# Loading the first x of a batched matmul: two row tiles in one buffer, and other pieces for the DMA engines

## Chip, cores, metric

The kernel runs on one core of a Trainium2 chip. The metric is the device time of one execution in microseconds (us). A run of this program on one core has no second core or die beside it to compare with; all runs below are listed as fast.

## What is computed

```python
batch, m, k, n = 32, 512, 1024, 768
x:      float32 [32, 512, 1024]
weight: float32 [32, 1024, 768]
out = np.matmul(x, weight)         # float32 [32, 512, 768]
```

Reading and writing this once is 167.8 MB in and 50.3 MB out.

## The kernel before

Weights and all x but the first are cast to bf16 by the DMA itself, on a queue that POOL issues (queue 0 in the profile). The first x comes as float32 on the queue of SP (queue 1), in two buffers: three row tiles in one transfer, the fourth tile in seventeen pieces. The tile is 128 partitions, one row of 4 KB in each.

```python
x_first = x_pool.tile([P, MT - 1, K], F32, name="x_sb")
x_fourth = one_pool.tile([P, 1, K], F32, name="one_sb")
nc.sync.dma_start(x_first, x_view[0, :, :MT - 1])
few = [slice(at, first + 20, 4) for first in (0, 20, 40) for at in range(first, first + 4)]
for rows in (slice(64, 96), slice(96, 112), slice(112, P), slice(60, 62), slice(62, 64), *few):
    nc.sync.dma_start(x_fourth[rows, 0], x_view[0, rows, MT - 1])
load_w(0)
# ... identity
load_pair(1); load_w(1); load_w(2); load_pair(3)
```

Each entry of `few` is a transfer of five rows. A transfer of five rows runs on fewer DMA engines than one of 128 (the prediction cites the page for this and shows packets that come in fives), so the pieces set how much each DMA engine carries.

The order of work in a batch: x is transposed on PE, DVE copies the transposed tile from PSUM, PE multiplies, ACT and DVE take the result out, POOL issues the store. Before batch b POOL issues the weights of batch b + 3, and must wait there until PE has done with the buffer that they go to.

```python
for b in range(B):
    if b % 2 and b + AHEAD + 1 < B:
        load_pair(b + AHEAD + 1)       # cut: the last one
    if b % 2 and 2 < b < B - HELD - AHEAD:
        store((b - 3) // 2)
    if b + AHEAD < B:
        load_w(b + AHEAD)
    # ... transposes
    for pair in range(2):              # two row tiles each
        for half in range(2):
            mt = 2 * pair + half
            if mt not in xT:
                xT[mt] = transpose_first(mt)     # batch 0: the late tiles
            matmuls(pm, half, xT[mt], b, range(KT), False)
        evacuate(b, pair, pm)
```

## Time and profile before

| | before |
|---|---|
| time, three runs | 514.83 us (514.74 to 515.25); the profiled run, a fourth, 514.44 |
| span in the profile | 512.7 us |
| PE busy | 435.4 us |
| sum of PE's three waits for DMA | 55.6 us (26.2 for weights, 19.1 and 10.3 for the first x) |

The lines behind this table stand in the prediction. How to read them: in the windows, the column before the last is the mean busy share of the sixteen DMA engines (it reads 1.02 to 1.03 over long stretches here, as packets of one engine overlap a little), and the last is what they moved. A packet is counted whole in the window in which it starts. In a window of 1 us, about as long as one packet of queue 0, the share is therefore rough; at the end of the run, where packets take 0.23 us, it is good. A share of one engine alone is 1/16, or 0.06.

A second reading comes from the packet records that the trace keeps: start, length, size and queue of every DMA packet, without the number of the engine. Each transfer ends on each engine that it ran on with a completion packet of 4 bytes. The last transfers of the kernel are even over all engines, eight packets of 6,144 bytes on each, so the completions of one engine follow each other at 1.85 us, and a completion with none 1.85 us after it is the end of one engine. I call these times the finishes. They are worked out from the records by that rule. The shares of the last windows check them: a finish at 508.4 us takes 0.6 of a sixteenth off the window from 508 to 509.

### The profile page before, as it was taken

How to read it: one execution, taken by the hardware profiler on the slowest of the kernel's cores; microseconds unless marked ns; L12 is line 12 of the kernel's file. 1: busy time of each engine (PE TensorE's matmuls, PEld its weight loads, DVE VectorE, ACT ScalarE, POOL GpSimd, SP SyncE). 2: the span in 40 equal slices, each digit the busy share in tenths (PEclk: the TensorE clock that was granted, in tenths of full speed). 3: DMA queues.
4: the chain of work that ended last, by engine and by line, in shares of the span. 5: the costliest groups of instructions: out<-in, count | busy, mean ns of one | idle time of the engine just before them, and what ended most of it. 6: DMA issues, size and time to landing. Idle time of an engine off the chain costs nothing.

```text
span 512.7 us, 5785 instructions
## 1 busy us (share of the span) xinstructions
PE 435.4 (85%) x2576; PEld 278.7 (54%) x2576; DVE 130.0 (25%) x196; ACT 76.1 (15%) x129; POOL 39.1 (8%) x73
## 2 busy tenths in 40 slices
PE   1806999999999996997989989798898989999991
PEld 1504666666666663654646546464464645666660
DVE  0202324141515141320413205041040410514121
ACT  1100121212121201111111111111101111120201
POOL 3000010101010101001010000101001000010000
PEclk9956999999999998997999989899798998999997
DMA  8999999999999999999999999999999999999998
GB/s 240 224 221 213 218 220 216 333 221 310 243 218 336 215 324 231 228 325 220 330 223 234 318 223 334 217 247 304 221 333 218 258 295 220 331 215 212 320 427 345
DMA packets 12712, 135.63 MB, mean 265 GB/s; under 512 B 1296, under 2 KB 1296, under 8 KB 3088
## 3 DMA queue, kind: packets, MB, share of 16 engines
q0 software_dynamic: 11440, 126.88, 96.6%
q1 hardware_dynamic: 1248, 8.39, 4.1%
q8 instruction: 20, 0.33, 0.2%
q14 instruction: 4, 0.03, 0.0%
HBM read 167.77 MB, written 50.33 MB: 425 GB/s over the span
## 4 chain that ended last, share of the span: by engine, by line
PE 46%; DMA 37%; issue 8%; DVE 5%; another core or an unknown queue 1%; POOL 1%; ACT 0%; SPq 0%; POOLq 0%
PE pm L123 40%; DMA w_sb<-in_weight_dram 28%; DMA one_sb<-in_x_dram 8%; PE pt L78 5%; DVE xT L85 4%; DVE out_sb L144 1%; POOL out_dram L164 0%; PE pt L105 0%; POOL w_sb L70 0%; POOL x_sb L60 0%; DVE one_sb L144 0%; DVE xT L93 0%; ACT out_sb L145 0%; SPq L151 0%
## 5 line engine op out<-in xcount | busy, mean ns | idle before, releaser
L123 PE MATMUL pm<-w_sb,xT 128*128 128x256 bf16 (+1 forms) x2048 | 353.7, 336 | 26.4 <-DMA w_sb<-in_weight_dram 26.2
L123 PEld LDWEIGHTS <-xT 128*128 128x128 bf16 x2048 | 205.3, 101 | 170.3 <-DMA w_sb<-in_weight_dram 29.3
L144 DVE COPY out_sb<-pm 128x512 f32<-128x512 f32 x62 | 42.9, 691 | 317.6 <-PE pm L123 317.6
L78 PE MATMUL pt<-ident,x_sb 128*128 128x128 f32 x496 | 79.8, 302 | 10.5 <-DVE xT L85 10.2
L78 PEld LDWEIGHTS pt<-ident,x_sb 128*128 128x128 f32 x496 | 69.3, 209 | 21.5 <-DVE xT L85 18.7
L85 DVE COPY xT<-pt 128x1024 bf16<-128x1024 bf16 x120 | 77.4, 687 | 11.0 <-PE pt L78 11.0
L143 ACT COPY out_sb<-pm 128x512 f32<-128x512 f32 x62 | 36.3, 585 | 271.7 <-PE pm L123 271.7
L145 ACT COPY out_sb<-pm 128x512 f32<-128x512 f32 x62 | 36.3, 585 | 145.7 <-PE pm L123 145.6
L70 POOL DMA_DIRECT2D w_sb<-in_weight_dram x37 | 20.1, 544 | 404.8 <-PE pm L123 397.6
L105 PE MATMUL pt<-ident,one_sb 128*128 128x128 f32 x8 | 1.9, 421 | 19.1 <-DMA one_sb<-in_x_dram 19.1
L106 DVE CAST xT<-pt 128x512 bf16<-128x512 f32 x8 | 5.8, 733 | 34.6 <-PE pt L105 34.1
L105 PE MATMUL pt<-ident,x_sb 128*128 128x128 f32 x24 | 5.3, 383 | 10.5 <-DMA x_sb<-in_x_dram 10.3
L105 PEld LDWEIGHTS pt<-ident,one_sb 128*128 128x128 f32 x8 | 1.6, 219 | 19.4 <-issue 19.4
L164 POOL DMA_DIRECT2D out_dram<-out_sb x14 | 10.1, 719 | 6.7 <-ACT out_sb L143 3.5
L105 PEld LDWEIGHTS pt<-ident,x_sb 128*128 128x128 f32 x24 | 4.1, 209 | 11.5 <-issue 10.3
L60 POOL DMA_DIRECT2D x_sb<-in_x_dram x15 | 8.1, 539 | 10.9 <-DMA w_sb<-in_weight_dram 10.9
L144 DVE COPY one_sb<-pm 128x512 f32<-128x512 f32 x2 | 1.4, 690 | 9.0 <-PE pm L123 9.0
L93 DVE COPY xT<-pt 128x1024 bf16<-128x1024 bf16 x4 | 2.6, 686 | 0.2 <-PE pt L78 0.2
L143 ACT COPY one_sb<-pm 128x512 f32<-128x512 f32 x2 | 1.2, 585 | 6.4 <-PE pm L123 6.4
L145 ACT COPY one_sb<-pm 128x512 f32<-128x512 f32 x2 | 1.2, 585 | 1.6 <-PE pm L123 1.6
L143 ACT ACT_TABLE_LOAD x1 | 1.3, 1283 | 0.7 <-PEq L232 0.7
L64 POOL DMA_DIRECT2D x_sb<-in_x_dram x1 | 0.5, 528 | 2.1 <-DMA w_sb<-in_weight_dram 2.1
(6 smaller groups left out, 0.9 us busy)
## 6 DMA issues: line engine op xcount, KB each, us to landing
w_sb<-in_weight_dram POOLq DMA_DIRECT2D x28, 1536.0 KB, 41.7
out_dram<-out_sb POOLq DMA_DIRECT2D x14, 3072.0 KB, 55.3
x_sb<-in_x_dram POOLq DMA_DIRECT2D x15, 2048.0 KB, 49.8
w_sb<-in_weight_dram POOLq DMA_DIRECT2D x7, 768.0 KB, 38.2
out_dram<-out_sb SPq DMA_DIRECT2D x2, 1536.0 KB
x_sb<-in_x_dram SPq DMA_DIRECT2D x1, 1536.0 KB
out_dram<-one_sb SPq DMA_DIRECT2D x2, 768.0 KB
out_dram<-out_sb SPq DMA_DIRECT2D x2, 768.0 KB
```

The source lines that it names most:

```text
L60: nc.gpsimd.dma_start(out=xs[b], in_=pair_view[b // 2])
L70: nc.gpsimd.dma_start(out=ws[b][:, at:at + n, :], in_=w_view[b, :, at:at + n, :])
L78: nc.tensor.transpose(pt[:, j, :], pairs[:, mo, j::JT], ident)
L85: nc.vector.tensor_copy(both[:, :, :, :, half, :].rearrange("p b j i r -> p j b i r"), words(b, mt + MT * half).rearrange("p j (b i r) -> ...
L93: nc.vector.tensor_copy(xT.rearrange("p j m r -> p (j m r)"), words(B - 1, mt).rearrange("p j m -> p (j m)"))
L105: nc.tensor.transpose(pt[:, i, :], rows[:, JT * h + i::KT], ident)
L106: nc.vector.tensor_copy(xT[:, 2 * h:2 * h + 2].rearrange("p j m r -> p j r m"), pt.rearrange("p (j r) m -> p j r m", r=2),)
L123: nc.tensor.matmul(pm[bank][:, at:at + size], xT[:, ko // 2, :, ko % 2], ws[b][:, ko, off:off + size], start=(ko == 0 and not (together an ...
L143: nc.scalar.copy(o[:, 0:512], pm[0])
L144: nc.vector.tensor_copy(o[:, 512:1024], pm[1])
L145: nc.scalar.copy(o[:, 1024:N2], pm[2])
L164: nc.gpsimd.dma_start(out=two_view[at], in_=twos[at])
```

## The change

The first two tiles get a transfer each (a quarter of x[0] is enough for PE to begin), and the last two tiles share one buffer, so that a row of 8 KB can come in one packet. The pieces now are: 80 partitions in transfers of 16 spread partitions (two of five such transfers cut into halves of 4 KB), 8 partitions in one transfer, 40 in transfers of five.

```diff
-        x_first = x_pool.tile([P, MT - 1, K], F32, name="x_sb")
-        x_fourth = one_pool.tile([P, 1, K], F32, name="one_sb")
-        nc.sync.dma_start(x_first, x_view[0, :, :MT - 1])
-        few = [slice(at, first + 20, 4) for first in (0, 20, 40) for at in range(first, first + 4)]
-        for rows in (slice(64, 96), slice(96, 112), slice(112, P), slice(60, 62), slice(62, 64), *few):
-            nc.sync.dma_start(x_fourth[rows, 0], x_view[0, rows, MT - 1])
+        x_first = x_pool.tile([P, 2, K], F32, name="x_sb")
+        x_second = one_pool.tile([P, 2, K], F32, name="one_sb")
+        for mt in range(2):
+            nc.sync.dma_start(x_first[:, mt], x_view[0, :, mt])
+
+        def load_second(rows, *parts):
+            for tiles in parts:
+                nc.sync.dma_start(x_second[rows, tiles], x_view[0, rows, 2:][:, tiles])
+
+        whole, halves = (slice(0, 2),), (slice(0, 1), slice(1, 2))
+        for at in range(5):
+            load_second(slice(48 + at, P, 5), *(halves if at > 2 else whole))
+        load_second(slice(40, 48), *whole)
+        for first in (0, 20):
+            for at in range(first, first + 4):
+                load_second(slice(at, first + 20, 4), *whole)
```

Cut: `rows` in `transpose_first`, which follows the new buffers, and the number of tiles transposed ahead in batch 0, two in place of three.

More of the change, by code (lines that the diff above doesn't have):

```diff
@@ L100, in transpose_first @@
         xT = xT_pool.tile([P, JT, P, 2], BF16, name="xT")
-        rows = x_first[:, mt] if mt < MT - 1 else x_fourth[:, 0]
+        rows = x_first[:, mt] if mt < 2 else x_second[:, mt - 2]
         for h in range(2):
@@ L187 @@
             if b == 0:
-                xT = {mt: transpose_first(mt) for mt in range(MT - 1)}
+                xT = {mt: transpose_first(mt) for mt in range(2)}
             elif b == B - 1:
```

## The prediction

> **What bounds the kernel now.** I read the page first for the engines, slices and queues, then the chain of waits, then windows around both ends, then the waits of the SP queue, and last the single DMA packets that the trace records (start, length, size, queue).
>
> ```profile
> span 512.7 us, 5785 instructions
> PE 435.4 (85%) x2576; PEld 278.7 (54%) x2576; DVE 130.0 (25%) x196; ACT 76.1 (15%) x129; POOL 39.1 (8%) x73
> DMA  8999999999999999999999999999999999999998
> q0 software_dynamic: 11440, 126.88, 96.6%
> q1 hardware_dynamic: 1248, 8.39, 4.1%
> q8 instruction: 20, 0.33, 0.2%
> HBM read 167.77 MB, written 50.33 MB: 425 GB/s over the span
> ```
>
> The DMA row is at 9 in every slice but the first and last, and the shares of queues 0 and 1 sum to over 100%. The sixteen DMA engines are the bound. PE has 15% to spare. The arithmetic agrees: 218.1 MB over 16 engines is 13.63 MB each; a 12,288-byte packet of queue 1 alone takes 460 ns in the packet records, 26.7 bytes per ns; 13.63 MB at that rate is 510 us. So nothing that PE waits for counts unless it leaves a DMA engine without work.
>
> ```profile
> core 0: us, PE busy (x) PEld busy (x) DVE busy (x) ACT busy (x) POOL busy (x), PEclk, DMA share, GB/s
> 0.00:2.00 2.00, 0.00 (x0) 0.00 (x0) 0.00 (x0) 1.26 (x1) 0.93 (x6) 1.00 0.40 68
> 2.00:6.00 4.00, 0.00 (x0) 0.00 (x0) 0.00 (x0) 0.02 (x1) 3.09 (x7) 1.00 0.86 310
> 6.00:43.00 37.00, 13.34 (x73) 8.80 (x74) 5.06 (x7) 1.76 (x3) 0.53 (x1) 0.79 1.03 228
> 43.00:500.00 457.00, 420.29 (x2494) 269.02 (x2495) 123.51 (x187) 70.98 (x122) 34.52 (x60) 0.96 1.02 266
> 508.00:509.00 1.00, 0.00 (x0) 0.00 (x0) 0.00 (x0) 0.00 (x0) 0.00 (x0) 0.50 0.97 406
> 509.00:510.00 1.00, 0.00 (x0) 0.00 (x0) 0.00 (x0) 0.00 (x0) 0.00 (x0) 0.50 0.81 338
> 510.00:511.00 1.00, 0.00 (x0) 0.00 (x0) 0.00 (x0) 0.00 (x0) 0.00 (x0) 0.50 0.47 197
> 511.00:512.70 1.70, 0.00 (x0) 0.00 (x0) 0.00 (x0) 0.00 (x0) 0.00 (x0) 0.50 0.02 7
> ```
>
> These windows show where time can still be had: before 6 us, where the share is low, and after 508 us, where the engines run dry one after the other. In between the share is 1.02. At the end the last completion packets (4 bytes, 9 ns, one per engine) give each engine's own finish: three engines near 508.7 to 509.1 us, seven at 510.14 to 510.54, six at 510.98 to 511.41. Their mean is about 510.5, so a perfect balance would win 0.9 us, 0.2% of the time. That is the whole prize at that end.
>
> ```profile
> PE pt L105 <- DMA one_sb<-in_x_dram: 19.1, 1, 19.1
> PE pt L105 <- DMA x_sb<-in_x_dram: 10.3, 1, 10.3
> ```
>
> Both of these are PE waiting for the first x in the first 43 us (DMA share 1.03 from 6 us on). They look large and cost nothing. The chain of waits runs through the landing of one_sb at 42.9 us, but that chain is a dependency path, and no engine of the bound stands still beside it.
>
> **What the Trainium skill says.** "DMA: Bandwidth & Descriptors", Queues, rings and completion order: each DMA engine takes turns between the queues it has work for, one packet at a time. The trace agrees: on the engines that load the five-row pieces, a 172 ns data packet and a 22 ns completion packet alternate with queue-0 packets of 925 ns. The same page, the section on why a DMA increments its semaphore by 16: the row count fixes how many engines a transfer uses, and on SP it is the lowest-numbered ones; so 16 spread rows go to all sixteen engines, 8 to engines 0 to 7, 5 to engines 0 to 4. The trace agrees on the number: the late 4,096-byte packets come in fives, at 0, 9, 56, 142 and 154 ns; it carries no engine numbers. "Runtime: NRT & Kernel Launch", Instruction fetch mechanics: instructions arrive in blocks of 16 KiB by DMA. The trace has twenty such packets, queue 8, of 880 to 975 ns. Following packets by their phase, these went round eight engines that carry none of the five-row pieces: four engines get three, four get two. That reading is partly ambiguous where two phases meet.
>
> **The balance before.** Rows of x_first are even. The fourth tile puts 18 rows of 4 KB on engines 0 and 1, 16 on 2 to 4, 4 on 5 to 15. A 4 KB packet between queue-0 packets adds 168 ns (172 less 4 of overlap), so engines 0 and 1 carry 14 x 0.168 = 2.35 us more than 5 to 7, and engines 2 to 4 carry 2.0 us more. Fetches add 2 x 0.935 = 1.9 us or 3 x 0.935 = 2.8 us to eight engines, which I take to be 8 to 15. So three engines should be early (5 to 7), seven in the middle (2 to 4 and the four with two fetches), six late (0, 1 and the four with three fetches). These are the counts 3, 7, 6 read above.
>
> **The change, part by part.** No arithmetic changes: the same 8 x 4 transposes, the same copies, and the same POOL order; the SP queue still issues 18 loads at the start. What moves:
>
> - *First two tiles*: 16 packets of 4 KB per engine in place of eight of 12 KB (which held the third tile too). 4 KB alone costs 159 - 4 = 155 ns, so 16 x 0.155 = 2.48 us.
> - *Tiles 2 and 3 in one buffer.* A spread transfer leaves one partition per engine, 8 KB, or two of 4 KB for the two that are halved. An 8 KB packet was not in the trace; between 168 ns for 4 KB and 469 for 12 KB it should add 318 ns (estimate). Engines 0 to 4: 3 x 0.318 + 4 x 0.168 + 9 x 0.318 = 4.49 us; 5 to 7: 3 + 1 of the large, 1.94 us; 8 to 15: 1.63 us. A completion packet adds 3 ns, at most 18 of them.
> - *Sums of the loads of x[0]* after: 7.02 us on engines 0 to 4, 4.45 on 5 to 7, 4.13 on 8 to 15. Before, with 3.67 us for x_first: 6.75 on 0 and 1, 6.41 on 2 to 4, 4.36 on 5 to 15. Differences: +0.27, +0.61, +0.10, -0.23 us.
> - *Where each class then ends:* 0 and 1 from about 511.0 to 511.3; 2 to 4 from 510.1-510.5 to 510.8-511.1; the fetchers with three from 511.2-511.4 to 511.0-511.2; the rest earlier. The last end goes from 511.41 to some 511.2-511.3, a gain of 0.1 to 0.2 us.
>
> *The start.* DMA begins 1.0 us after the first SP issue in both. Until the first queue-0 packet at 6.0 us only queue 1 works, and moved 82 KB per engine there, where 4.2 us at 26.7 bytes per ns would be 110. After: the first two tiles hold 64 KB, and SP issues take 0.25 to 0.77 us, so six pieces (36 KB) are issued by about 5 us: 100 KB, enough. No change expected, within 0.3 us either way.
>
> *Beside the path.* PE needs only the first tile (512 KB) to begin, so its first transpose should come at some 6 us in place of 10.3. The first matmul waits for w[0] and stays near 16 us. Tiles 2 and 3 land when engines 0 to 4 are through: of their 50 turns some 28 are left at 6 us, against 37 of 44 before. 28 queue-0 packets (17 at 0.906, 8 at 1.208, the rest completions) are 25 us, with 94 KB of own data 3.7 us: 34.8 us, and PE goes on at about 35 in place of 42.9. It then has two tiles to transpose and multiply rather than one and a half, so batch 0 ends near 47 in place of 49. As DMA has a backlog there, it gains nothing.
>
> The sum: 514.83 - 0.2 = **514.6 us**.
>
> **The rivals.**
>
> *The earlier landing shortens the run* by the 2 us of batch 0 or the 7 us of PE's wait. For: the chain of waits passes there. Against: the share is 1.02 to 1.03 from 6 to 508 us, so the loads that PE's progress releases only join a queue. It would make 508 to 513. I give it 3%.
>
> *The start starves or small packets lose.* With pieces of one packet per engine issued about every 0.6 us, or with slow first packets (the first twelve took 750 to 1,650 ns in place of 460), all engines could lose 0.3 to 0.8 us before 6 us, and nothing later gives it back. It would make 515.0 to 515.5. Against: the backlog computed above. 20%.
>
> *The balance is better than I think*, if engines 0 to 4 were all in the middle group: then they rise to 510.4-511.1, the fetchers fall by 0.23, and the end is that 0.23 us earlier or slightly more: 514.3 to 514.6. This differs from my path only in the class of engines 0 and 1, which the trace doesn't name.
>
> **Range and chances.** The parts I dispute are each tenths of a microsecond, and three runs of before spread over 0.5 us. So 513.9 to 515.3 should hold it 8 times in 10. A change of 2% is 10 us, ten times what either end has to give: within 2% 0.98, faster 0.01, slower 0.01.
>
> **What would show it.** Right: share at 1.02 between 6 and 508 us; first transpose near 6 us, x_second's wait ending near 35 us; matmuls of batch 0 beginning near 16 us; the last finishes closer together, latest near 511.2, with three early engines still near 509. Wrong: a share under 0.8 between 2 and 6 us (start starved); a latest finish of five engines together after 511.4 (0 to 4 overloaded); a span shorter by over a microsecond, which would mean that PE's wait was paid for somewhere.

## The result

| | before | after |
|---|---|---|
| time, four runs each in the same rounds | 515.03 us (514.74 to 515.25) | 514.97 us (514.78 to 515.75) |
| ratio of the means | | 1.0002 (95%: 0.9985 to 1.0019) |
| sum of PE's waits for DMA | 55.6 us | 56.8 us |
| latest finish of a DMA engine | 511.4 us | 512.6 us (this run), 511.8 us (a second one) |

Ratios are the mean time of one kernel's runs over that of the other's of the same rounds, so not quite the ratio of the medians in the table. The change makes no difference that these runs can show. The profile of the changed kernel is of its slowest run, 515.75 us; the same kernel was profiled a second time, at 514.99 us, among the experiments.

The page of the changed kernel:

```profile
span 514.0 us, 5786 instructions
DMA  8999999999999999999999999999999999999997
q0 software_dynamic: 11440, 126.88, 96.4%
q1 hardware_dynamic: 1472, 8.39, 4.1%
q8 instruction: 20, 0.33, 0.2%
HBM read 167.77 MB, written 50.33 MB: 424 GB/s over the span
```

Queue 1 moves the same 8.39 MB in 224 packets more. The bytes, the bound and the instruction packets are unchanged.

The same windows as in the prediction, of the changed kernel (DMA share and GB/s are the last two columns):

```profile
0.00:2.00 2.00, 0.00 (x0) 0.00 (x0) 0.00 (x0) 1.26 (x1) 0.93 (x6) 1.00 0.07 16
2.00:6.00 4.00, 0.84 (x4) 0.88 (x5) 0.00 (x0) 0.02 (x1) 3.10 (x7) 1.00 1.00 303
6.00:43.00 37.00, 14.48 (x61) 8.53 (x60) 5.07 (x7) 1.17 (x2) 0.53 (x1) 0.68 1.03 231
43.00:500.00 457.00, 417.07 (x2495) 267.56 (x2494) 123.37 (x187) 71.40 (x122) 34.52 (x60) 0.96 1.02 266
509.00:510.00 1.00, 0.00 (x0) 0.00 (x0) 0.00 (x0) 0.00 (x0) 0.00 (x0) 0.50 0.79 332
510.00:511.00 1.00, 0.00 (x0) 0.00 (x0) 0.00 (x0) 0.00 (x0) 0.00 (x0) 0.50 0.57 240
511.00:512.00 1.00, 0.00 (x0) 0.00 (x0) 0.00 (x0) 0.00 (x0) 0.00 (x0) 0.50 0.31 129
```

In the first 6 us the DMA engines were busy for 2 x 0.07 + 4 x 1.00 = 4.14 us on the mean, against 2 x 0.40 + 4 x 0.86 = 4.24 before: the start is neither starved nor better. From 6 to 500 us the share is the same to the digit. At the end it is 0.31 between 511 and 512 us, where before it was nearly gone (0.02 from 511.00 to 512.70): in this run five engines on the mean are still at work in that microsecond.

PE's waits for DMA over the whole run, in us, number, longest; before and then after (two of the three of before stand in the prediction):

```profile
PE pm L123 <- DMA w_sb<-in_weight_dram: 26.2, 8, 4.5
```

```profile
PE pm L123 <- DMA w_sb<-in_weight_dram: 34.9, 10, 5.8
PE pt L105 <- DMA one_sb<-in_x_dram: 16.7, 1, 16.7
PE pt L105 <- DMA x_sb<-in_x_dram: 5.2, 1, 5.2
```

PE begins at 5.2 us in place of 10.3 and the second half lands earlier, so two waits shrink by 7.5 us together. The wait for weights grows by 8.7. In the second profile of the changed kernel the three sum to 55.5 us. This fits a wait that is not the bound: taken away at one place, it comes back at a later load.

The finishes, worked out from the packet records (us from the start of the span; "after, second" is run e1 below):

```
before         508.7 508.7 509.1 | 510.1 510.1 510.2 510.3 510.3 510.5 510.5 | 511.0 511.1 511.1 511.2 511.4 511.4
after          507.6 507.7 508.1 | 509.9 509.9 510.0 510.1 | 511.1 511.4 511.5 511.6 511.6 511.6 511.8 | 512.5 512.6
after, second  507.8 508.2 508.2 | 509.9 510.0 510.2 510.2 510.3 510.6 510.7 510.9 511.1 511.1 511.2 | 511.6 511.8
```

The mean of the sixteen is 510.4, 510.6 and 510.2 us. So in the second run nothing was lost or won in total, and the last engine ends 0.4 us later than before. In the first profiled run there is a disturbance besides: five packets at 121.6 us took 0.7 to 1.0 us longer than their like (x loads of 16,384 bytes, which otherwise take 1,227 ns). The second profile of this kernel has no such group there.

### The profile page after: what moved, and what is told of

Its sections match the earlier page's. It is cut to its first block, busy times and chain, and to the rows that moved or that the text cites. A ratio compares the mean times of both kernels' runs of the same rounds, so it can differ in the third digit from the quotient of the medians.

```text
span 514.0 us, 5786 instructions
## 1 busy us (share of the span) xinstructions
PE 435.9 (85%) x2576; PEld 278.9 (54%) x2576; DVE 129.8 (25%) x196; ACT 76.1 (15%) x129; POOL 39.1 (8%) x73
## 3 DMA queue, kind: packets, MB, share of 16 engines
q1 hardware_dynamic: 1472, 8.39, 4.1%
## 4 chain that ended last, share of the span: by engine, by line
PE 47%; DMA 35%; issue 8%; DVE 5%; another core or an unknown queue 1%; SPq 1%; POOL 1%; ACT 0%; POOLq 0%
PE pm L123 41%; DMA w_sb<-in_weight_dram 29%; DMA one_sb<-in_x_dram 6%; PE pt L78 5%; DVE xT L85 4%; DVE out_sb L144 1%; SPq L156 1%; PE pt L105 0%; POOL out_dram L174 0%; POOL x_sb L60 0%; POOL w_sb L70 0%; SPq L152 0%; DVE xT L106 0%; DVE one_sb L144 0%
## 5 line engine op out<-in xcount | busy, mean ns | idle before, releaser
L78 PE MATMUL pt<-ident,x_sb 128*128 128x128 f32 x496 | 79.8, 302 | 10.4 <-DVE xT L85 10.2
L78 PEld LDWEIGHTS pt<-ident,x_sb 128*128 128x128 f32 x496 | 69.3, 209 | 21.5 <-DVE xT L85 18.7
L105 PE MATMUL pt<-ident,one_sb 128*128 128x128 f32 x16 | 3.0, 350 | 16.7 <-DMA one_sb<-in_x_dram 16.7
L105 PE MATMUL pt<-ident,x_sb 128*128 128x128 f32 x16 | 3.9, 423 | 5.2 <-DMA x_sb<-in_x_dram 5.2
L105 PEld LDWEIGHTS pt<-ident,x_sb 128*128 128x128 f32 x16 | 3.0, 215 | 5.6 <-issue 5.1
## 6 DMA issues: line engine op xcount, KB each, us to landing
x_sb<-in_x_dram SPq DMA_DIRECT2D x2, 512.0 KB
```

The costliest lines, as they stand in the source:

```text
L78: nc.tensor.transpose(pt[:, j, :], pairs[:, mo, j::JT], ident)
L105: nc.tensor.transpose(pt[:, i, :], rows[:, JT * h + i::KT], ident)
```

## The experiments

Theory (balance): sixteen DMA engines are busy from 2 to 508 us; the time is the mean load plus the lead of the engine that ends last, and what the pieces do is to hand out load. Rival 1: PE's wait for the late half of x[0] counts. Rival 2: the many small transfers at the start cost. All kernels below gave correct results. All ratios are to the kernel before, in the same rounds; 515 us times 0.001 is 0.5 us. Where two experiments are compared, it is by these ratios, and their error is that of both.

### The changed kernel again (e1)

Edit: none.

> The changed kernel unaltered, timed beside the three others of this call on one chip. All theories: within 0.5 us of the kernel before (ratio 0.999 to 1.001). Balance theory: per-engine finishes again three early (near 508 to 509 us), four near 510, the rest from 511.1 on.

Measured: 514.99 us (514.91 to 515.41) against 514.61 (514.39 to 515.20) of the kernel before; ratio 1.0009 (0.9996 to 1.0021). The time is as expected. Of the finishes the three early ones are there; the others lie between 509.9 and 511.8 us with hardly a gap, not in the two groups expected. If there is a difference in time, the change is the slower one.

### The wait taken away: one even transfer (e2)

```diff
-        (all pieces of x_second)
+        nc.sync.dma_start(x_second, x_view[0, :, 2:])
```

> Tiles 2 and 3 of the first x come in one transfer of 128 partitions, so all sixteen engines get the same rows, and the piece-wise loading is gone. Balance theory (DMA engines are the bound, the run ends with the last of them): PE's wait for the second half of x[0] shrinks from 16.8 us to under 2 us, and yet the run becomes longer by 0.4 to 1.0 us than the changed kernel, because the engines with instruction fetches get 24 KB each back (3 x 0.318 us). The finishes should fall into groups of eight (no fetch, earliest), four (two fetches, some 1.9 us later) and four (three fetches, some 2.8 us later than the first). Rival 1 (PE's wait counts): 2 us faster or more. Rival 2 (many small SP transfers starve the start): faster by 0.3 to 0.8 us, as three transfers take the place of 18.

Measured: 516.60 us (516.47 to 516.86), ratio 1.0039 (1.0025 to 1.0053), so 1.5 us slower than the changed kernel by the difference of the ratios, where 0.4 to 1.0 had been expected. The order of PE's work in that run (start, length, what; in brackets the wait before it):

```profile
5.28 3.89 PE L105 MATMUL pt<-ident,x_sb 128*128 128x128 f32 x16 [5.28 <-DMA x_sb<-in_x_dram]
16.17 7.80 PE L123 MATMUL pm<-w_sb,xT 128*128 128x512 bf16 x32 [7.00 <-DMA w_sb<-in_weight_dram]
23.81 1.05 PE L105 MATMUL pt<-ident,one_sb 128*128 128x128 f32 x8
25.46 2.55 PE L123 MATMUL pm<-w_sb,xT 128*128 128x256 bf16 x15 [0.60 <-DVE xT L106]
```

PE goes from the first half to the second without any wait: the 16.7 us are gone, and the run is longer. Over the run it then waits for weights instead:

```profile
PE pm L123 <- DMA w_sb<-in_weight_dram: 45.0, 14, 7.0
```

Rival 1 falls, at least for this landing and that of the changed kernel. Of rival 2 nothing is seen: three transfers in place of eighteen brought no gain that would outweigh the imbalance. The finishes fall into the groups that were expected, with wider steps:

```
even   508.4 508.6 508.6 508.8 508.8 509.2 509.6 509.6 | 510.8 511.3 511.6 511.8 | 512.1 512.7 512.8 513.1
```

Eight engines end at 509.0 on the mean, four at 511.4, four at 512.7, though all carry the same data. The pieces exist to level this. The mean of all sixteen is 510.5 us, against 510.2 in the changed kernel (e1), and the last finish 513.1 against 511.8: the time follows the last engine. The steps are 2.4 and 3.7 us, where two and three instruction fetches were to account for 1.9 and 2.8. If the fetches make the steps (4 x 2 + 4 x 3 are the twenty of the trace), one costs its engine some 1.2 us rather than the 0.935 of its packet. (The expectations further down still use a first reading of 509.2 for the early group.)

### More rows on the first five engines (e3)

```diff
-        for at in range(5):
-            load_second(slice(48 + at, P, 5), *(halves if at > 2 else whole))
-        load_second(slice(40, 48), *whole)
-        for first in (0, 20):
+        for at in range(3):
+            load_second(slice(80 + at, P, 3), *whole)
+        for first in (0, 20, 40, 60):
```

> 80 partitions instead of 40 come in five-row transfers, 48 spread, none in the transfer of eight. Balance theory: engines 0 to 4 carry 40 KB (5 x 0.318 = 1.6 us) more than in the changed kernel and end last, alone, as a group of five; the run is 1.2 to 1.8 us longer; all other engines end earlier, and the share of the last 2 us falls to about 5/16. Rival 1 (PE's wait counts): the second half lands some 17 us later (16 more turns), so the run is longer by 5 us or more. Rival 2 (balance doesn't matter, only the start): within 0.3 us.

Measured: 518.60 us (518.18 to 520.37), ratio 1.0082 (1.0068 to 1.0096): 3.8 us slower than the changed kernel, twice what the balance gives. And not five engines ended late but thirteen, at 513.1 to 514.7 us. The second half landed only 6 us later, at 46 us, and yet something was lost there. The windows of that run:

```profile
71.00:72.00 1.00, 1.00 (x9) 0.61 (x7) 0.00 (x0) 0.00 (x0) 0.00 (x0) 1.00 0.59 123
72.00:73.00 1.00, 1.00 (x7) 0.52 (x6) 0.69 (x1) 0.59 (x1) 0.39 (x1) 1.00 0.35 74
```

Laid over time, the packet records have 6.7 and 6.0 packets under way on the mean in the two microseconds from 72 us on (16.3 elsewhere), so an engine lost 1.4 us on the mean between 70 and 76 us. My theory knew nothing of this. And the finishes show no imbalance left at the end: their mean is 513.2 us, 2.9 later than in e1, and the last is 1.5 us after the mean, where in e1 it is 1.6. The loss is common to all engines. Perhaps the engines with more rows caught up while the others stood idle; no record names the engines, so that is not shown.

### The late landing alone (e6)

The same late landing without the rows: three of the eight five-row transfers are cut into 4 KB halves.

```diff
-                load_second(slice(at, first + 20, 4), *whole)
+                load_second(slice(at, first + 20, 4), *(halves if first == 20 and at > 20 else whole))
```

> The changed kernel with three of its eight five-row transfers halved into 4 KB pieces: six more turns on engines 0 to 4, no other bytes (0.05 us more on those engines). Theory of the dry queue: the second half of x[0] lands near 46 us as in the run with 80 five-row partitions, PE ends batch 0 some 6 us later than in the changed kernel, POOL issues the loads that wait for PE too late, and the DMA share falls under 0.6 for 1 to 3 us between 70 and 76 us; all sixteen engines end later by the same amount and the run is 1.5 to 3 us longer than the changed kernel. Pure balance theory: within 0.3 us of the changed kernel.

Measured: 517.58 us (515.98 to 518.58), ratio 1.0058 (1.0042 to 1.0074), 2.5 us slower than the changed kernel. PE went on at 45.97 us, as wanted. Two windows of this run, columns as before, and the first of them in the changed kernel (e1); then from the timeline POOL's issues of weights in this run and the one that answers to the second of them in e1, with start, length and in brackets the wait before:

```profile
72.00:73.00 1.00, 1.00 (x8) 0.61 (x7) 0.12 (x1) 0.23 (x1) 1.00 (x3) 1.00 0.53 115
73.00:74.00 1.00, 1.00 (x8) 0.61 (x7) 0.00 (x0) 0.00 (x0) 0.67 (x1) 1.00 1.14 184
```

```profile
72.00:73.00 1.00, 1.00 (x8) 0.55 (x6) 0.69 (x1) 0.59 (x1) 0.00 (x0) 1.00 0.88 184
```

```profile
55.84 0.53 POOL L70 DMA_DIRECT2D w_sb<-in_weight_dram  x1 [46.09 <-PE pm L123]
71.91 0.53 POOL L70 DMA_DIRECT2D w_sb<-in_weight_dram  x1 [15.54 <-PE pm L123]
```

```profile
67.34 0.53 POOL L70 DMA_DIRECT2D w_sb<-in_weight_dram  x1 [15.54 <-PE pm L123]
```

This is how the dip comes about: POOL may issue the next weights only when PE has freed a buffer; with PE 4.6 us later it issues at 71.91 us, and by then the DMA engines have worked off what they had. The changed kernel issued at 67.34 us, and its engines were busy all through (its 0.88 is an effect of counting by starts; the packet records have 16.3 packets under way there, as elsewhere). The dip was shallower than the 0.6 for 1 to 3 us that I had written: in e6 the records have 13.4 and 11.7 packets under way in the two windows shown, and an engine lost some 0.5 us on the mean.

So the dry queue is not most of the loss. All sixteen engines do end later, by 2.3 us on the mean (510.2 to 512.5), as the theory had it. But from 88 us on, with the engines busy, 28 packets of x loads (16,384 bytes) were slow and took up to 3.0 us in place of 1.23. That is 1.5 us for each engine on the mean, and another 0.3 us lies in packets of weights just after the dip; the three parts make 2.3 us, and the profiled run is 2.2 us slower than that of e1. The same slow x packets cost 1.5 us in e3 and 0.9 to 1.5 in the other runs in which PE went on at 43.7 us or later (e7, e10, e11), 0.6 in e8, and no more than 0.3 at that place in the rest. So large losses of this kind come with a late landing; what makes the packets slow is not shown. A window of e3 has them: a full share, but 180 GB/s, where x loads otherwise move some 215:

```profile
90.00:91.00 1.00, 1.00 (x9) 0.66 (x7) 0.00 (x0) 0.09 (x1) 0.00 (x0) 1.00 1.34 180
```

PE's wait in batch 0 is thus free when PE goes on at 40 us (e1) or, with less left to do, at 42.9 (the kernel before, whose share is 1.01 from 60 to 100 us), and costs real time at 46. The loss in e3 (3.2 us between the profiled runs) is of the same kind: 1.4 us of idle engines, 1.5 in slow x packets, 0.4 in packets of weights, and by its finishes no imbalance that is left.

### The imbalance alone, attempted (e7)

The same rows as in e3, but the first two tiles in one transfer, which was to bring the second half in earlier.

```diff
-        for mt in range(2):
-            nc.sync.dma_start(x_first[:, mt], x_view[0, :, mt])
+        nc.sync.dma_start(x_first, x_view[0, :, :2])
         (pieces as in e3)
```

> The 80 five-row partitions again (the same bytes on each engine as in the run that was 4 us slower than the kernel before), but the first two tiles come in one transfer of 8 KB packets: nine turns in place of eighteen, so the second half lands near 37 to 41 us. Theory that the loss had two parts: no dip of the DMA share near 72 us, only engines 0 to 4 late (40 KB, 1.6 us more than in the changed kernel), so 0.7 to 1.6 us longer than the changed kernel. If the imbalance alone made the loss: 3.5 us longer again.

Measured: 517.94 us (517.82 to 519.03), ratio 1.0069 (1.0055 to 1.0082). The experiment missed its aim: PE went on at 45.2 us, not at 37 to 41, and the share fell to 0.29 between 72 and 73 us. The mistake was in the count of turns: the packets of the first two tiles pass before queue 0 has work, so their number hardly delays anything (PE went on 0.9 us earlier than in e3). It says nothing about the imbalance alone.

### The changed kernel with its first two tiles in one transfer (e8)

Edit: the first two lines of e7 only.

> The changed kernel with its first two tiles in one transfer (8 KB packets) instead of one for each tile (4 KB packets): the part of the change that lets PE begin at 5.2 us taken back. All theories that hold DMA for the bound: PE begins near 7 to 8 us, the second half lands earlier (nine turns fewer), and the time is within 0.3 us of the changed kernel. If the early start of PE is worth something: slower by 1 us or more; if 4 KB packets cost at the start: faster by 0.3 us or more.

Measured: 515.54 us (514.89 to 516.61, four runs), ratio 1.0019 (1.0006 to 1.0033). PE began at 6.8 us and went on at 38.0. The median is 0.55 us above that of e1, but the runs spread over 1.7 us and the fastest of both are alike (514.89 and 514.91). Inconclusive; no gain was seen. The profile is of the slowest of these runs: one engine ended alone at 513.4 us, while the mean of the sixteen was 510.4. Each engine carries the same bytes as in e1, where the last ended at 511.8, in larger packets; and the two profiles of the changed kernel itself differ by 0.8 us in the last finish. So tenths in a single profile mean little.

### Which engines carry the fetches (e4, e5, e9, e10, e11)

I had taken engines 5 to 7 for free and 8 to 15 for those with fetches. Then transfers of eight rows are the right tool, and this should have been the best of all (in this section the lines shown take the place of all pieces of `x_second`):

```diff
+        for at in range(4):
+            load_second(slice(64 + at, P, 4), *whole)
+        for first in range(0, 64, 8):
+            load_second(slice(first, first + 8), *whole)
```

> 64 partitions spread over 16 engines (32 KB each), 64 in transfers of eight (64 KB on each of engines 0 to 7), none in fives. Balance theory: engines 5 to 7, which end 2 to 3 us before the others, take 48 KB more; 0 to 4 have 16 KB less (-0.6 us), 8 to 15 have 8 KB less (-0.3 us). No early group of three any more; the finishes lie within 1.5 us; the run is 0.3 to 0.7 us shorter than the changed kernel, and the fastest of the four. Rival (the three early engines are not 5 to 7 but carry fetches): one or more engines end later than 512, and the run is 0.5 us longer or more.

Measured: 516.41 us (515.62 to 516.68), ratio 1.0030 (1.0017 to 1.0043). The rival of this expectation came true: an engine ended alone at 513.1 us, another at 512.0, and two at the early end, at 508.0. (I had first read one early engine, and the next expectation rests on that.) Then seven rows at a time, to leave engine 7 out:

```diff
+        for at in range(3):
+            load_second(slice(80 + at, P, 3), *whole)
+        for first in range(0, 77, 7):
+            load_second(slice(first, first + 7), *whole)
+        load_second(slice(77, 80), *whole)
```

> 48 partitions spread (24 KB on every engine), 77 in transfers of seven, three in one of three: engines 0 to 6 carry 112 KB of tiles 2 and 3 (0 to 2: 120), 7 to 15 carry 24. Revised balance theory, from the groups of the even run and the two odd engines of the run with transfers of eight (one late alone, one early alone): engine 7 has instruction fetches and engine 15 has none. Then 0 to 6 end near 511.2, the engines with three fetches near 511.1 (scatter 0.5), those with two near 509.8, one engine alone near 507.6; no engine after 511.8; time 0.2 to 0.6 us under the changed kernel, about that of the kernel before. First balance theory (5 to 7 without fetches, 8 to 15 with): the same, but engine 7 would be the early one. If engine 5 or 6 has fetches, it ends alone near 513.4 or later.

Measured: 516.61 us (515.69 to 517.33), ratio 1.0035 (1.0021 to 1.0049). Two engines ended at 513.4 and 513.5 us. Missed again, by the third case that I had written down: engines among 5 and 6 have fetches. To count rather than guess, three kernels put 128 KB more on a set of eight, seven or six engines than on the rest:

```diff
+        for first in range(0, 128, 8):                      # e9
+            load_second(slice(first, first + 8), slice(0, 2))
```

> All of tiles 2 and 3 in sixteen transfers of eight rows: 128 KB on engines 0 to 7, none on 8 to 15, so that the two sets part by 5 us and can be counted. From the even run (engines without fetches at 509.2 with 64 KB, with two 511.4, with three 512.7; 0.04 us for each KB): an engine of the set without fetches ends near 511.8, one with them at 513.9 to 515.3, the rest by 510.5. If engines 5 to 12 fetch: three engines late, five in the middle. If only 5 and 6 of the set fetch: two late. If 8 to 15 fetch, as predicted at first: none late, eight in the middle.

```diff
+        load_second(slice(112, P), slice(0, 2))              # e10
+        for first in range(0, 112, 7):
+            load_second(slice(first, first + 7), slice(0, 2))
```

> As before with sets of seven: 16 rows spread, 112 in sixteen transfers of seven rows, 144 KB on engines 0 to 6, 8 KB less than 16 on the others. Without fetches 512.4, with them 514.6 to 515.9. If engines 5 to 12 fetch: two engines late, five in the middle, nine early. If 8 to 15 fetch: none late.

```diff
+        for first in (96, 112):                              # e11
+            load_second(slice(first, first + 16), slice(0, 2))
+        for first in range(0, 96, 6):
+            load_second(slice(first, first + 6), slice(0, 2))
```

> Sets of six: 32 rows spread, 96 in sixteen transfers of six rows, 144 KB on engines 0 to 5, 16 KB on the others. If engines 5 to 12 fetch: one engine late near 514.6 to 515.9, five near 512.4. If 8 to 15 fetch: none late, six near 512.4.

The tails of e11 (six), e10 (seven) and e9 (eight), in windows of 1 us with the columns as before:

```profile
515.00:516.00 1.00, 0.00 (x0) 0.00 (x0) 0.00 (x0) 0.00 (x0) 0.00 (x0) 0.50 0.06 25
516.00:517.00 1.00, 0.00 (x0) 0.00 (x0) 0.00 (x0) 0.00 (x0) 0.00 (x0) 0.50 0.06 25
```

```profile
515.00:516.00 1.00, 0.00 (x0) 0.00 (x0) 0.00 (x0) 0.00 (x0) 0.00 (x0) 0.50 0.12 49
516.00:517.00 1.00, 0.00 (x0) 0.00 (x0) 0.00 (x0) 0.00 (x0) 0.00 (x0) 0.50 0.10 43
```

```profile
514.00:515.00 1.00, 0.00 (x0) 0.00 (x0) 0.00 (x0) 0.00 (x0) 0.00 (x0) 0.50 0.15 61
515.00:516.00 1.00, 0.00 (x0) 0.00 (x0) 0.00 (x0) 0.00 (x0) 0.00 (x0) 0.50 0.12 49
```

With sets of six one engine works alone for two microseconds (0.06 is 1/16), with sets of seven two do (0.12 is 2/16). A transfer of six rows reaches engines 0 to 5 by the rule quoted in the prediction. None of 0 to 4 can be the one: in e1 they carry 48 KB more than in e2, so with two fetches one of them would have ended near 513 us there (an estimate: the 511.4 of e2 and 1.9 us), and the latest ended at 511.8. So the one is engine 5, and the two are 5 and 6. With sets of eight, two are clear and a third at 514.5 us lies 0.7 us behind the group before it, which leaves engine 7 open. The early engines speak on it: two in e4, where 8 to 15 carry little, and three in e5 (508.1 to 508.2 us), where 7 to 15 do. By these counts engine 7 has no fetches, two of 8 to 15 have none either, and the fetches fall on 5, 6 and six of 8 to 15. All this is inferred from counts of finishes. (In e10 the set carries 136 KB, not the 144 of the expectation; the difference of 128 KB stands.) The times (518.89, 520.66 and 520.04 us, two runs each) mean nothing for the question, as the second half landed at 42.6 to 45.8 us and the queue ran dry in part. In e9 and e10 the engines outside the set have a common finish (eight of e9 within 511.7 to 511.8 us). The last stores were issued only at 507.0 and 509.0 us there (501.7 in e1), so these engines had to wait for them; that the late engines held up the last weights and so PE is my guess, not shown.

### Without the transfer of eight rows (e12)

If 5 and 6 carry fetches, the transfer of eight in the change loads engines that are already late.

```diff
-        load_second(slice(40, 48), *whole)
-        for first in (0, 20):
-            for at in range(first, first + 4):
-                load_second(slice(at, first + 20, 4), *whole)
+        load_second(slice(45, 48), *whole)
+        for first in range(0, 45, 5):
+            load_second(slice(first, first + 5), *whole)
```

> The changed kernel without its transfer of eight rows: 45 rows in fives, three in one of three, 80 spread as they are. If engines 5 to 7 carry fetches, the transfer of eight put 8 KB (0.32 us) on engines that end last; without it the last of them ends 0.3 us earlier, 0 to 2 take 0.32 us more and stay under 511.5: 0.1 to 0.4 us faster than the changed kernel, level with the kernel before or a little under it. If 5 to 7 are the early engines: 0 to 0.3 us slower than the changed kernel.

Measured: 515.21 us (515.12 to 515.54) against 514.55 (514.41 to 514.78), ratio 1.0014 (1.0000 to 1.0028). The latest finish was 511.6 us, 0.2 under that of e1, which says little (see e8), and the time shows no gain over the changed kernel; by the ratios it is 0.25 us above, well inside the error. So what the transfer of eight costs can't be told apart from nothing. No kernel beats the kernel before.

## Why the prediction was right, point by point

**The bound: right.** The DMA share between 6 and 500 us is 1.02 to 1.03 in both kernels. Taking PE's 16.7 us wait away made the run longer (e2).

**"Nothing that PE waits for counts unless it leaves a DMA engine without work": right, and the condition was nearer than I thought.** The rival of the earlier landing was held down by this, correctly. But I wrote of "a backlog" there without asking how deep it is. It is a few microseconds deep: POOL's second issue at 67.3 us is harmless, at 71.9 us it comes too late (e6). The idle engines cost some 0.5 us of the 2.5 by which that run is longer; most of the rest is packets that were slow later, at 88 us and after.

**The landing of tiles 2 and 3 at 34.8 us: mechanism right, size off.** PE went on at 39.2 us. The term that was mis-sized is what queue 1 gets done before queue 0 begins: I had assumed 82 KB per engine by 6.0 us as before, and it was 58 KB by 5.1 us, so 33 or so turns were left in place of 28. The same sum with these numbers (9 + 9 + 9 + 5 or 6 turns of queue 0, 28.8 to 29.7 us, and 118 KB of own data, 4.7 us) gives 38.6 to 39.5; the last completion was at 38.7. The prediction named the landing as beside the path, so the time was not touched.

**Batch 0 ending near 47 us: off.** POOL's first load that waits for batch 0 was issued at 49.3 us against 49.5 before, as PE had more left to do and did it at a granted clock of 0.50 between 36 and 43 us, after its pause. The first matmul, which I had left near 16 us, came at 14.8; queue 0 had begun at 5.1 us in place of 6.0.

**The 8 KB packet at 318 ns: right.** It took 322 ns, of which 4 overlap.

**The start: right in what it costs.** Busy DMA time in the first 6 us was 4.14 us after and 4.24 before. The 100 KB for each engine by 6 us were 64, as queue 0 began earlier and shared the engines.

**The balance, "-0.23 us" for the engines with fetches and a gain of 0.1 to 0.2 us: this step failed.** Its premise was the set of engines with fetches, "which I take to be 8 to 15", and "5 to 7" as the three early ones. The counts of three, seven and six fitted, but they fit other sets as well. By e10, e11 and the finishes of e1, engines 5 and 6 have fetches; by e4 and e5, 7 and two of 8 to 15 are the early ones. For 5 and 6 the change adds 8 KB (+0.10 us by my own sum) where I took 0.23 us off, so the latest finish need not fall. It did not: 511.8 us in the undisturbed profile, where I had said near 511.2, and 511.4 before. Which engine was the last is not shown, and 0.10 us doesn't explain 0.4; but the two profiles of this kernel differ by more than that. My sign of being wrong, five engines together after 511.4, came in the first of them (eight did, in the run with the disturbance) and not in the second (two). The fetch was also too small in the sum: 1.2 us by the groups of e2, not 0.935. And the mean of the finishes before is 510.4 us, not 510.5, so the prize was 1.0 us, not 0.9.

**The rivals and the range.** The starved start did not come. "The balance is better than I think" did not come either. That the time fell into the range is in part luck. The prize at the end bounds what a change of pieces can win, but not what it can lose: e4 and e5, built on wrong sets, were 1.8 and 2.0 us slower than the kernel before. This change moved only 8 KB onto each of 5 and 6, so the wrong set cost nothing that the runs can tell.

What stays open: which six of 8 to 15 carry fetches, why x packets are slow from 88 us on after a late landing, and whether the change is truly a few tenths of a microsecond slower: both intervals (1.0002 and 1.0009 in the middle) hold 1.

## What to carry to other kernels

Where the DMA engines are busy from start to end, look at the last microseconds engine by engine: the sum of bytes may be fixed while one engine ends 4 us after another, as in e2. What better pieces could win in the kernel before was the lead of the last engine over the mean, 1.0 us; what worse ones lost was 1.8 to 2.0 us (e4, e5). A wait of another engine is free only as long as the queue has work behind it, so ask how many microseconds deep it is before calling a wait harmless. And when a count of engines supports an assignment, make a run that separates the sets widely before building on it: two "best" kernels here were built on a wrong set, and three runs with 128 KB of difference settled most of it.

## What the Trainium skill lacked or had wrong

- "Runtime: NRT & Kernel Launch", Instruction fetch mechanics, calls the fetch hidden behind instruction issue. Nothing here tests that for the engines that compute, but in a kernel bound by DMA the fetch takes its time from one data engine: twenty blocks of 16 KiB, each some 1.2 us on its engine by the groups of the even run (finishes at 509.0, 511.4 and 512.7 us). No page says which engines serve it; here, by the same groups, eight of the sixteen do, 5 and 6 among them.
- "DMA: Bandwidth & Descriptors", Rules for kernel authors, advises transfers over all sixteen engines. Here the even transfer was the slower one, 516.60 us against 514.99 for the pieces of the changed kernel: the engines' other load is uneven, and the last engine ended at 513.1 us against 511.8.
- "DMA: Bandwidth & Descriptors", Queues, rings and completion order, gives the turn-taking by packets, and the runs agree. What it lacks is the consequence: a transfer on one queue beside a full other queue lands after as many packets of the other queue as it has packets and completions, at 0.9 to 1.2 us each. Six turns more moved the landing from 40 to 46 us (e1 to e6).
